# q and k as eight pairs by seven products, with all value columns ahead of them

## The chip, the cores and the metric

The kernel runs on one core of a Trainium2 chip. The metric is device time in microseconds (us) of one launch. The engines are named PE (TensorE, the matmul engine), DVE (VectorE), ACT (ScalarE), POOL (GpSimd) and SP (SyncE, which here only issues DMA transfers).

## The reference, cut to what matters

One step of a hybrid layer on 1024 prompt tokens and 64 new tokens of running streams (T = 1088 columns): an input projection feeds a state-space scan and a differential attention, and a gated mix and a convolutional feed-forward network (FFN) follow. The part that the change touches is

```python
xn = rmsnorm(x) ; proj = xn @ w_in                     # D_MODEL = 1024
z, xbc, dt_raw, q, k, v, gate_ssm, gate_att = split(proj)
q = rope(rmsnorm_per_head(q, q_norm_w))                # 16 heads of 64, q and k 1024 wide each
k = rope(rmsnorm_per_head(k, k_norm_w))                # k is also an output of the step
...
o = diff_attention(q, k_all, v_all)                    # needs all of q, k, v and the cached keys
```

All products are in float32: each operand is split into a high and a low float32r part, and a product is three matmuls (hi hi, lo hi, hi lo) into the same PSUM tile.

## The kernel before, in words

Everything is kept transposed: features on the 128 partitions, the 1088 tokens in the free dimension. `xn` is the normed input, eight feature tiles (KT = 8), held in SBUF as high and low parts in three column ranges `WIDE` of 384, 384 and 320. `weights` loads a block of weights (`w_f`), casts it on ACT (`w_hi`) and subtracts on DVE (`w_lo`). `project` then forms one block of 128 output rows: for each column range 8 x 3 matmuls (L148 to L150) into one bank from `acc`, and a callback `evac` that empties the bank. One call of `next` on it is a "piece" (24 matmuls). A Tile scheduler puts the program into an order for each engine; `tc.high_priority` moves some steps ahead.

The stages, in the order of the program:
1. The input norm, in six column slices (`NORM`); the square sums go over PE (L254). As soon as the first slices are ready, `values(0)` and `values(1)` form the first half of v, together with the raw dt columns.
2. `steps()` turns dt into the decay tables `nacum, decs, dt_tok, dtw` that the scan needs much later; they stay in SBUF.
3. `heads(B_Q, ...)`: the eight row blocks of q one after the other. `evac` copies the bank into a row `qr` in SBUF, squares it on ACT (L325) and adds the square to `ss` on DVE (L326). After the last block a matmul with the block matrix `blk` sums over each head (L335), `rstd_of` (L210 to L214) makes the inverse root, and `finish` multiplies each row (L343), rotates the first two (rope, L352 to L357), splits it (`split_out`: cast on ACT L307, subtraction on DVE L308) and stores the two parts to `q_st`. All rows stay in SBUF meanwhile.
4. `values(2)`, `values(3)`: the other half of v, and the split of the cached keys.
5. `heads(B_K, ...)`: the same for k, which is also stored plain to the output `kT` (L339), then as two parts to `k_st` (L310).
6. Attention, eight heads of nine units (`attend`); head_tiles fetches `q_t, kh_t, kl_t` and others for a head from DRAM (L492). `kh_t` of any head holds rows from all eight row blocks of k, so the first score matmul (L534) comes after the last store of k. Between units `fill(ATT_STEPS)` puts pieces of plain projections (gates `g`, `z`, and the convolution's `xBC`, in `ORDER`) from one stream into PE's queue; they do not depend on attention, and what the stream still has is taken up in the scan. The scheduler also sets plain pieces between k's last product and the first score.
7. The scan, the branches, the output projection, and the FFN, which in both kernels forms its products by a Strassen-Winograd scheme: seven products of half size for eight, 272 columns wide (QW = T / 4).

## Time and profile before

| | |
|---|---|
| median of 3 runs | 2492.93 us (2492.44 to 2493.63) |
| the profiled execution's own time | 2499.35 us |
| its span, first to last instruction | 2497.2 us |
| mean granted clock of PE | 0.993 |
| busy: PE, DVE, ACT, POOL | 2441.4, 1592.7, 1181.6, 691.4 us |
| DMA | 403.62 MB, mean 162 GB/s |

A row of the grouped view reads: line, engine, operation, output<-input, shape, xcount, then busy us and mean ns of one, then the idle time of that engine before them and what ended it. A window's row has for each engine the busy time and (xcount) of its instructions, then the granted clock, the DMA engines' busy share and GB/s. A timeline row has start, duration, engine, line and operation. A row of DMA issues has count, KB of one and the median us from issue to landing. The records of matmuls overlap, since the engine is pipelined: how fast they follow each other is read from their starts or from their number in a full window, not from the duration of one.

### The profile page before, as it was taken

How to read it: one execution, taken by the hardware profiler on the slowest of the kernel's cores; microseconds unless marked ns; L12 is line 12 of the kernel's file. 1: busy time of each engine (PE TensorE's matmuls, PEld its weight loads, DVE VectorE, ACT ScalarE, POOL GpSimd, SP SyncE). 2: the span in 40 equal slices, each digit the busy share in tenths (PEclk: the TensorE clock that was granted, in tenths of full speed). 3: DMA queues.
4: the chain of work that ended last, by engine and by line, in shares of the span. 5: the costliest groups of instructions: out<-in, count | busy, mean ns of one | idle time of the engine just before them, and what ended most of it. 6: DMA issues, size and time to landing. Idle time of an engine off the chain costs nothing. (4 is left out here: it accounts for less than half of the span.)

```text
span 2497.2 us, 44757 instructions
## 1 busy us (share of the span) xinstructions
PE 2441.4 (98%) x16958; PEld 2361.0 (95%) x16958; DVE 1592.7 (64%) x2735; ACT 1181.6 (47%) x2564; POOL 691.4 (28%) x712
## 2 busy tenths in 40 slices
PE   8999999999999999999999999899999999999998
PEld 7999999999999999998889899899999999999998
DVE  7326255865777667537666773655687777777765
ACT  6234343644665555437646663325543333344541
POOL 3000000100111001004324331003466676766435
PEclk9999999999999999999999999999999999999999
DMA  5217248454355353255688753755234343457874
GB/s 166 78 56 272 81 190 277 138 163 142 115 152 144 111 152 107 90 189 171 200 286 272 248 162 108 242 181 175 70 110 141 122 141 123 133 186 217 221 181 152
DMA packets 272152, 403.62 MB, mean 162 GB/s; under 512 B 32544, under 2 KB 206240, under 8 KB 271808
## 3 DMA queue, kind: packets, MB, share of 16 engines
q1 hardware_dynamic: 267328, 391.85, 49.0%
q0 software_dynamic: 4608, 8.91, 2.4%
q8 instruction: 133, 2.18, 0.4%
q14 instruction: 83, 0.68, 0.1%
HBM read 267.11 MB, written 133.56 MB: 160 GB/s over the span
## 5 line engine op out<-in xcount | busy, mean ns | idle before, releaser
L148 PE MATMUL mm<-xn_hi,w_hi 128*128 128x384 f32 (+1 forms) x1416 | 469.9, 332 | 0.9 <-DVE zr L430 0.9
L150 PE MATMUL mm<-xn_hi,w_lo 128*128 128x384 f32 (+1 forms) x1416 | 467.7, 330 | 0.4 <-DVE w_lo L142 0.4
L149 PE MATMUL mm<-xn_lo,w_hi 128*128 128x384 f32 (+1 forms) x1416 | 466.5, 329 | 0.0
L148 PEld LDWEIGHTS mm<-xn_hi,w_hi 128*128 128x128 f32 x1416 | 266.2, 188 | 5.3 <-issue 2.0
L150 PEld LDWEIGHTS mm<-xn_hi,w_lo 128*128 128x128 f32 x1416 | 266.1, 188 | 2.9 <-issue 0.8
L149 PEld LDWEIGHTS mm<-xn_lo,w_hi 128*128 128x128 f32 x1416 | 266.2, 188 | 1.8 <-issue 0.6
L142 DVE TENSOR_TENSOR w_lo<-w_f,w_hi 128x1024 fp32r<-128x1024 f32 (+1 forms) x120 | 151.6, 1264 | 129.5 <-ACT w_hi L141 128.6
L1037 PE MATMUL mx<-n,wh 128*128 128x272 f32 x1092 | 209.5, 289 | 2.1 <-ACT u L1173 1.5
L1037 PE MATMUL mx<-m,w_hi 128*128 128x272 f32 x1050 | 202.8, 290 | 6.4 <-DVE down L1187 3.8
L141 ACT CAST w_hi<-w_f 128x1024 fp32r<-128x1024 f32 (+1 forms) x120 | 125.8, 1049 | 128.6 <-PE mm L149 75.2
L1037 PEld LDWEIGHTS mx<-n,wh 128*128 128x128 f32 x1092 | 171.9, 189 | 2.7 <-ACT u L1173 1.7
L1037 PEld LDWEIGHTS mx<-m,w_hi 128*128 128x128 f32 x1050 | 166.9, 190 | 7.6 <-DVE down L1187 4.2
L1037 PE MATMUL mx<-n,wl 128*128 128x272 f32 x546 | 157.6, 289 | 0.0
L148 PE MATMUL mm<-b_hi,w_hi 128*128 128x384 f32 (+1 forms) x448 | 148.0, 331 | 8.5 <-DVE b_g L192 5.3
L1037 PE MATMUL mx<-m,w_lo 128*128 128x272 f32 x525 | 152.4, 290 | 0.0
L150 PE MATMUL mm<-b_hi,w_lo 128*128 128x384 f32 (+1 forms) x448 | 146.8, 328 | 0.0
L149 PE MATMUL mm<-b_lo,w_hi 128*128 128x384 f32 (+1 forms) x448 | 146.7, 327 | 0.0
L548 ACT ACTIVATE p_t<-sc,mx 128x1024 f32<-128x1024 f32 (+5 forms) x144 | 106.1, 739 | 74.9 <-DVE mx L539 36.7
L459 DVE SCALAR_TENSOR_TENSOR cc<-pre,par,cc 128x384 f32<-128x384 f32 (+1 forms) x216 | 126.6, 586 | 22.9 <-ACT cc L457 17.8
L447 POOL COPY pre<-pre 128x3 f32<-128x3 f32 x48 | 13.2, 274 | 453.7 <-ACT pre L448 330.4
L686 POOL TENSOR_SCALAR_AFFINE_SELECT bc<-bc 128x1024 f32<-128x1024 f32 (+1 forms) x36 | 39.7, 1104 | 261.4 <-ACT e L673 261.4
L840 ACT CAST w_hi<-ws 128x512 fp32r<-128x512 f32 (+1 forms) x64 | 38.8, 607 | 150.9 <-PE mx L1037 106.7
(375 smaller groups left out, 6759.9 us busy)
## 6 DMA issues: line engine op xcount, KB each, us to landing
w_f<-in_win_dram SPq DMA_DIRECT2D x76, 512.0 KB, 3.8
w_f<-in_wup_dram SPq DMA_DIRECT2D x44, 512.0 KB, 3.7
hr<-q_sc SPq DMA_DIRECT2D x70, 272.0 KB, 4.3
bc<-a_sc SPq DMA_DIRECT2D x32, 512.0 KB, 5.8
q_sc<-hb SPq DMA_DIRECT2D x44, 272.0 KB, 2.3
gb<-q_sc SPq DMA_DIRECT2D x44, 272.0 KB, 3.7
x_sc<-cc SPq DMA_DIRECT2D x48, 192.0 KB, 2.2
q_sc<-gb SPq DMA_DIRECT2D x33, 272.0 KB, 2.3
```

Of the source, the lines that this page charges most:

```text
L141: S.copy(hi, w)
L142: V.tensor_tensor(out=lo, in0=w, in1=hi, op=ALU.subtract)
L148: PE.matmul(ps, a_hi, b_hi, start=i == 0, stop=False)
L149: PE.matmul(ps, a_hi, b_lo, start=False, stop=False)
L150: PE.matmul(ps, a_lo, b_hi, start=False, stop=i == n - 1)
L447: G.tensor_copy(pre[:, 0:3], tail)
L459: V.scalar_tensor_tensor(cc[:, :m], pre[:, i : i + m], cw(i), cc[:, :m], ALU.mult, ALU.add)
L548: act(p_t[:n, :nk], sc[c][:n, :nk], AF.Exp, bias=mx[:n, c : c + 1], accum_out=dst)
L686: G.affine_select(bc[:L, :, :L], bc[:L, :, :L], [[0, 8], [1, L]], ALU.is_ge, -1e30, base=0, channel_multiplier=-1)
L840: S.copy(hi, src)
L1037: PE.matmul(ps, w[x][:, c], b[y][:, k], start=start and k == t == 0, stop=k == nk - 1 and t == 2, skip_group_check=not start)
```

## The change

**Values first.** `values(2)` and `values(3)` follow `values(0)` and `values(1)` directly, with the dt steps. `xn` becomes one pair of tiles [128, 8, 1088] instead of three pairs by column range.

**q and k by seven products.** The sixteen row blocks are taken as eight pairs. For each pair `left_blocks` loads the two weight blocks, forms the four sums of the scheme on POOL and splits seven left factors (`split`: ACT, then DVE). The right factors are quarters of `xn` (`X`: b11, b21, b22) and four differences t1 to t4, formed once by `differences` beside the values (nine operations on DVE and three on POOL, on 128x544, four times) and split too. There is no room for t1: it goes to DRAM (`t_sc`), and then takes the place of xn's quarter b12, which is kept in `b_sc` and restored during the last pair (`fourth`). `seven` runs the products, each twice 12 matmuls of 272 columns (L575), and adds the parts in the evacuations (L554, L585, L589).

**Rows go through DRAM.** A finished half row `pre` is squared (ACT), summed (now on POOL) and stored to `r_sc`. `Heads.finish` does the norm (L509 and `rstd_of` on 272 columns), then for 16 half rows: load `raw` (L514; the pool `mid` has two of these tiles), multiply (L516, L518), store the plain row for k (L520), split, store both parts (L524). q's 16 units are stepped seven to a pair beside k's first pairs; k's come after the last pair, beside plain pieces. The split of the cached keys is stepped beside q's pairs.

**Plain pieces.** `fill(FIRST)`, twelve pieces, comes ahead of attention, and `ATT_STEPS` falls from 1.9 to 1.74, so that the total is the same. The dt tables are stored to `d_sc` and loaded again for the scan.

```diff
-ATT_STEPS = 1.9
+ATT_STEPS = 1.74
+FIRST = 12
+LEFT = dict(fa=8, fs=2)
+MID = dict(fu=4, pr=4, cc=4, ss=4, fr=2)
...
-        heads(B_Q, lambda j: wq8[:, j : j + 1], q_st, None)
-        run(values(2))
-        run(values(3))
-        for j in range(KT):
-            ck = row("ck", PAST)
-            load(out=ck, in_=ckT[P * j : P * (j + 1), :])
-            split_out(ck, j, PAST, c_st)
-        heads(B_K, lambda j: col(O_KN + j), k_st, kT)
+        load(out=d_sc, in_=dts.rearrange("p a b c -> p (a b c)"))
...
+        f12, f11 = whole("f12", 0, 2 + s, V), whole("f11", 0, s, G)
+        V.tensor_tensor(out=f11, in0=f12, in1=f11, op=ALU.subtract)
+        f22 = whole("f22", 1, 2 + s, V)
+        t2 = trow("t2f")
+        V.tensor_tensor(out=t2, in0=f22, in1=f11, op=ALU.subtract)
+        part("t2", t2)
+        G.tensor_tensor(out=f12, in0=f22, in1=f12, op=ALU.subtract)
+        part("t3", f12)
+        f21 = whole("f21", 1, s, G)
+        V.tensor_tensor(out=f21, in0=f21, in1=t2, op=ALU.subtract)
+        part("t4", f21)
...
+    for s in range(2):
+        for j in range(2):
+            differences(s, j)
...
+    for f in (2, 3):
+        run(values(f))
...
+        def squares(self, h, t):
+            if h not in self.ss:
+                self.ss[h] = mrow("ss", "ss")[:, :HALF]
+                act(self.ss[h], t, AF.Square)
+            else:
+                sq = mrow("cc", "sq")[:, :HALF]
+                act(sq, t, AF.Square)
+                G.tensor_tensor(out=self.ss[h], in0=self.ss[h], in1=sq, op=ALU.add)
...
+            for h in range(2):
+                for j in range(KT):
+                    x = mrow("fr", "raw")[:, :HALF]
+                    load(out=x, in_=r_sc[self.kind][P * j : P * (j + 1), HALF * h : HALF * (h + 1)])
+                    if j < 2:
+                        V.tensor_tensor(out=x, in0=x, in1=self.ss[h], op=ALU.mult)
+                    else:
+                        V.scalar_tensor_tensor(x, x, self.wcol(j), self.ss[h], ALU.mult, ALU.mult)
+                    if self.plain is not None:
+                        load(out=self.plain[P * j : P * (j + 1), HALF * h : HALF * (h + 1)], in_=x)
+                    hi, lo = (mrow("cc", n, R32)[:, :HALF] for n in ("qh", "ql"))
+                    split(hi, lo, x)
+                    for u, t in enumerate((hi, lo)):
+                        load(out=self.to[D * u + P * j : D * u + P * (j + 1), HALF * h : HALF * (h + 1)], in_=t.bitcast(F32))
+                    yield
...
+        for p, s in begin if n == 0 else both:
+            u.send((p, s))
+            if s == 1:
+                nxt += [x for x in [next(coming, None)] if x is not None]
+                next(finishing, None)
+            if n + 1 == len(order) and (p, s) == (4, 1):
+                fourth(b_sc)
+        left = nxt + list(coming)
+        if (kind, f) == ("q", 6):
+            finishing = chain(finishing, heads["q"].finish())
...
+    run(heads["k"].finish())
+    fill(FIRST)
```

How the order on the engines changes is shown at three places. First PE after k's last product; `ss` is the sum of squares, L335 and L509 are the statistics matmuls. Before:

```order
L150 MATMUL mm<-xn_hi_89,w_lo 128x320
L335 MATMUL st<-ss,con 128x384
L148 MATMUL mm<-xn_hi_85,w_hi 128x384
L149 MATMUL mm<-xn_lo_86,w_hi 128x384
L150 MATMUL mm<-xn_hi_85,w_lo 128x384
L148 MATMUL mm<-xn_hi_85,w_hi 128x384
L149 MATMUL mm<-xn_lo_86,w_hi 128x384
L335 MATMUL st<-ss,con 128x384
```

And with the change:

```order
L575 MATMUL mx<-xn_lo,w_hi 128x272
L575 MATMUL mx<-xn_hi,w_lo 128x272
L509 MATMUL mm<-ss,con 128x272 x2
L509 MATMUL mx<-ss,con 128x272 x2
L156 MATMUL mx<-xn_hi,w_hi 128x384
L157 MATMUL mx<-xn_lo,w_hi 128x384
L158 MATMUL mx<-xn_hi,w_lo 128x384
```

All four statistics matmuls now stand directly behind the last product, with no plain matmul between. Up to the first score matmul, 371 plain matmuls follow; before it was 448.

Second SP, in the middle of k's finish (`g_sc`, `z_sc` and `w_f` are the plain pieces' stores and weights). Before:

```order
L310 DMA k_st<-ql 128x1088
L310 DMA k_st<-qh 128x1088
L339 DMA out_dram<-qr 128x1088
L310 DMA k_st<-ql 128x1088
L431 DMA z_sc<-zr 128x384
L339 DMA out_dram<-qr 128x1088
```

And with the change:

```order
L520 DMA out_dram<-raw 128x544
L524 DMA k_st<-qh 128x544
L520 DMA out_dram<-raw 128x544
L524 DMA k_st<-ql 128x544
L524 DMA k_st<-qh 128x544
L514 DMA raw<-r_k 128x544
L524 DMA k_st<-ql 128x544
L652 DMA z_sc<-zr 128x384
L514 DMA raw<-r_k 128x544
```

The stores are half as wide and twice as many, and between them stand loads of `raw`, each of which needs its tile free, that is the plain store (L520) of two units earlier landed.

Third DVE in the pairs of k (L356 is a split's subtraction, L554 and L589 evacuate a bank). Before there were only the sums of squares and the weight remainders, like

```order
L326 TENSOR_TENSOR ss<-ss,qsq 128x384 x2
L142 TENSOR_TENSOR w_lo<-w_f,w_hi 128x1024
L326 TENSOR_TENSOR ss<-ss,qsq 128x320
L326 TENSOR_TENSOR ss<-ss,qsq 128x384 x2
L326 TENSOR_TENSOR ss<-ss,qsq 128x320
```

With the change, in k's last pair:

```order
L589 TENSOR_TENSOR u_3917<-mx,u_3917 128x272
L518 SCALAR_TENSOR_TENSOR raw<-raw,wq_1847,ss 128x544
L356 TENSOR_TENSOR ql<-raw,qh 128x544
L518 SCALAR_TENSOR_TENSOR raw<-raw,wq_1847,ss 128x544
L356 TENSOR_TENSOR ql<-raw,qh 128x544
L150 TENSOR_TENSOR w_lo<-w_f,w_hi 128x1024
L554 TENSOR_TENSOR pre<-mx,u_3917 128x272 x4
```

Units of q's finish, which wait for their `raw` loads, stand ahead of the evacuations of the pair.

More of the change, by code (lines that the diff above doesn't have):

```diff
@@ L409, in hybrid_layer @@
+    for s in range(2):
+        for j in range(2):
+            differences(s, j)
+    for u in range(2):
+        load(out=b_sc[P * u : P * (u + 1), :].rearrange("p (a t) -> p a t", a=4), in_=xn[u][:, :4, HALF:].bitcast(F32))
+    for f in (2, 3):
+        run(values(f))
+    tt.release()
     s1.close()
-    more = None, 0
-    ahead = AHEAD
+    st.release()
     extra.release()
     extra = None
-    cv_pool = tc.alloc_tile_pool(name="cv", bufs=1, side="right")
+    lp = tc.alloc_tile_pool(name="lp", bufs=1)
@@ new lines, in seven, with pile @@
+    def seven(to, left):
+        u1, u2 = to.u1, to.u2
+        banks = {}
+        def pile(key, p, s, start):
+            if start:
+                banks[key, s] = acc(QW)
+            ps, w, b = banks[key, s], left[p], X[PARTS[p], s]
+            for k in range(4):
+                c = slice(P * k, P * (k + 1))
+                for i, (x, y) in enumerate(((0, 0), (0, 1), (1, 0))):
+                    PE.matmul(ps, w[x][:, c], b[y][:, k], start=start and k == i == 0, stop=k == 3 and i == 2,
+                              skip_group_check=not start)
+            return ps
+        at = yield
+        for _ in range(14):
+            p, s = at
+            if p == 0:
+                S.copy(u1[:, s], pile("a", p, s, True))
+            elif p == 1:
+                V.tensor_tensor(out=u2[:, s], in0=pile("b", p, s, True), in1=u1[:, s], op=ALU.add)
+            elif p == 2:
+                to.take(0, 0, s, pile("a", p, s, False), None)
+            elif p == 3:
+                V.tensor_tensor(out=u1[:, s], in0=pile("b", p, s, False), in1=u1[:, s], op=ALU.add)
+            elif p == 4:
+                to.take(1, 1, s, pile("c", p, s, True), u1)
+            elif p == 5:
+                to.take(1, 0, s, pile("d", p, s, True), u1)
+            else:
+                to.take(0, 1, s, pile("c", p, s, False), u2)
+            at = yield
@@ L653, in hybrid_layer @@
         more = psi, 1
+        dts = sp.tile([P, 4, 9, 32], F32, name="dts")
+        nacum, decs, dt_tok, dtw = (dts[:, i] for i in range(4))
+        dtt = dts[:, 2:]
+        load(out=dts, in_=d_sc.rearrange("p (a b c) -> p a b c", a=4, b=9))
         def fetch(g, c, w):
```

274 lines of the change are left out of this document (194 added, 80 removed).

## The prediction

> **What bounds the kernel now.** I read the page's engine table first, then windows over the stages that the change touches, then the waits of TensorE (PE) there.
>
> ```profile
> PE 2441.4 (98%) x16958; PEld 2361.0 (95%) x16958; DVE 1592.7 (64%) x2735; ACT 1181.6 (47%) x2564; POOL 691.4 (28%) x712
> ```
>
> PE is busy 98 % of the span and no other engine passes 64 %. So the change is worth what it takes off PE, minus what it leaves PE waiting for. The windows (columns as their header line says, PE first) tell how full PE is in each stage.
>
> ```profile
> core 0: us, PE busy (x) PEld busy (x) DVE busy (x) ACT busy (x) POOL busy (x), PEclk, DMA share, GB/s
> 84.80:99.90 15.10, 15.10 (x92) 14.61 (x91) 8.92 (x18) 1.83 (x4) 0.00 (x0) 1.00 0.42 148
> 182.00:235.00 53.00, 53.00 (x437) 52.31 (x436) 35.01 (x38) 23.63 (x40) 0.00 (x0) 1.00 0.71 259
> 240.00:320.00 80.00, 80.00 (x488) 80.00 (x487) 20.55 (x30) 26.07 (x54) 0.10 (x1) 1.00 0.26 91
> 325.00:410.00 85.00, 83.63 (x499) 81.68 (x498) 47.15 (x66) 33.39 (x51) 0.00 (x0) 1.00 0.73 262
> 350.00:390.00 40.00, 38.68 (x233) 38.09 (x232) 30.19 (x35) 13.26 (x18) 0.00 (x0) 1.00 1.02 389
> 410.00:1099.00 689.00, 686.02 (x4405) 659.66 (x4404) 466.91 (x1010) 372.91 (x936) 48.33 (x143) 1.00 0.46 137
> 2000.00:2100.00 100.00, 100.00 (x800) 100.00 (x799) 72.14 (x103) 39.13 (x70) 69.25 (x67) 1.00 0.42 138
> ```
>
> Values 2 and 3 run at 182 to 235, the k products at 240 to 320, k's norm, split and stores at 325 to 410, attention at 410 to 1099; 2000 to 2100 lies in the FFN, which already uses seven products of 272 columns. PE idles only in k's finish (1.4 us in 85) and in attention (3.0 in 689). The DMA engines are full at one place: 350 to 390, share 1.02, 389 GB/s. The k finish is hidden at present, and I needed to see how. SP's and PE's timelines (start, duration):
>
> ```profile
> 388.46 0.32 SPq L310 DMA_DIRECT2D k_st<-ql  x1
> 397.00 1.50 SPq L492 DMA_DIRECT2D q_t<-q_st  x3
> 398.55 2.52 SPq L492 DMA_DIRECT2D kh_t<-k_st  x4
> 408.29 0.39 PE L534 MATMUL sc<-kh_t,q_t 128*128 128x512 f32 x1
> ```
>
> The last split store of k is issued at 388.46, the first head's keys are fetched from 398.55, and the first score matmul is at 408.29, 9.7 us after that fetch began. Between k's last product (about 330) and that score PE works through 448 plain matmuls. They cover it with only this left:
>
> ```profile
> PE mm L148 <- DVE zr L430: 0.9, 1, 0.9
> PE mm L150 <- DVE w_lo L142: 0.4, 1, 0.4
> ```
>
> **The change, part by part.** *The products.* Each old block of q or k is 72 matmuls of 384 or 320 columns, 16 blocks make 1152. By the window 240:320 one takes 80.00/488 = 163.9 ns, so 188.8 us. Each pair is now 7 products x 2 halves x 12 matmuls of 272 columns, eight pairs make 1344; by the window 2000:2100 one takes 100/800 = 125.0 ns, so 168.0 us. Gain **-20.8 us**. An eighth less arithmetic would be 23.6; the rest is lost because a narrow matmul costs more per column (0.460 against about 0.452 ns). A lost record in either window moves this by about 1 us.
>
> *The start.* PE's order now has 16 statistics matmuls of 192 columns ahead of the first value product, before 8.
>
> ```profile
> 15.03 2.12 PE L254 MATMUL st<-nsq,con 128*128 128x192 f32 x8 [0.43 <-ACT nsq L253]
> 17.38 1.83 PE L254 MATMUL st<-nsq,con 128*128 128x192 f32 x8 [0.23 <-ACT nsq L253]
> 19.74 0.40 PE L148 MATMUL mx<-w_hi,xn_hi 128*128 128x272 f32 x1 [0.53 <-ACT w_hi L141]
> ```
>
> One slice of the norm is 2.35 us (15.03 to 17.38), during which nothing else is ready: **+2.4**, between 0 (the slices that overlap products later get shorter by as much) and 5 (two slices).
>
> *The differences, beside values 2 and 3.* They must be ready when the first pair starts; the cover is the 53.0 us of those values, while q's 8 blocks used to lie between. VectorE gets 4 x 9 operations on 128x544, the dt steps (the window 84.80:99.90 holds only these on DVE, 8.92) and three weight remainders; GpSimd gets 12 additions.
>
> ```profile
> L352 DVE TENSOR_TENSOR t<-qr,rp x4: 718/718/720, 205.7 to 364.8; 128x544 f32<-128x544 f32 x4
> L142 DVE TENSOR_TENSOR w_lo<-w_f,w_hi 128x1024 fp32r<-128x1024 f32 x116 | 146.4, 1263 | 129.5 <-ACT w_hi L141 128.6 <-DMA out_dram<-x 0.5
> L1008 POOL TENSOR_TENSOR ge<-gb,gb 128x544 f32<-128x544 f32 x11 | 15.4, 1404 | 15.0 <-DMA gb<-q_sc 15.0
> L1011 POOL TENSOR_TENSOR gb<-gb,gb 128x544 f32<-128x544 f32 x11 | 18.8, 1705 | 0.8
> L841 DVE TENSOR_TENSOR w_lo<-ws,w_hi 128x512 fp32r<-128x512 f32 x56 | 47.8, 854 | 4.7 <-ACT w_hi L840 2.1
> L841 DVE TENSOR_TENSOR w_lo<-w_f,w_hi 128x512 fp32r<-128x512 f32 x28 | 41.3, 1476 | 3.8 <-ACT w_hi L840 3.8
> L841 DVE TENSOR_TENSOR wl<-w_f,wh 128x512 fp32r<-128x512 f32 x84 | 76.7, 914 | 19.3 <-ACT wh L840 18.7
> ```
>
> DVE: 36 x 0.718 + 8.92 + 3 x 1.263 = 38.6 us. POOL: 12 x 1.55 (between 1.404 and 1.705) = 18.6. Side by side that is under 53. But the three L841 rows show one operation on one shape at 854, 914 and 1476 ns, the slow form where POOL is adding to the same weights: the two engines hold each other up. Laid end to end they are 57.2, and the rest of dt (about 2 us of copies) follows: 59.2 - 53.0 = **+6**, between 0 (they overlap) and 14 (the first pair's four weight sums on POOL and four splits come behind as well). The Trainium skill, "SBUF — State Buffer", section "Who interferes with whom", says that a VectorE operation with two SBUF inputs and a GpSimd operation that reads SBUF wait for each other whole. By that rule alone this term is the +6, by plain overlap it is 0; the 1476 agrees with it, the 854 shows that it seldom hits.
>
> *q's finish, beside k's pairs.* The norm no longer works on rows that lie in SBUF. Sixteen half rows are read back from DRAM into two `raw` tiles, and VectorE's queue holds the multiply, which waits for that load, ahead of the pair's evacuations. Rows for the loads and stores (count, KB, median us to landing) and for the cast:
>
> ```profile
> hr<-q_sc SPq DMA_DIRECT2D x70, 272.0 KB, 4.3
> xr<-out_dram SPq DMA_DIRECT2D x16, 272.0 KB, 5.6
> out_dram<-down SPq DMA_DIRECT2D x16, 272.0 KB, 2.2
> out_dram<-x SPq DMA_DIRECT2D x32, 136.0 KB, 3.2
> kh_t<-k_st SPq DMA_DIRECT2D x32, 272.0 KB, 8.0
> ...
> L1024 ACT CAST m<-hr 128x544 fp32r<-128x544 f32 x40 | 25.5, 647 | 13.6 <-DMA hr<-q_sc 13.4
> ```
>
> A tile of q turns over in load 4.3, multiply 0.72, cast 0.65 and remainder 0.72: 6.4, up to 7.7 with a load of 5.6. Two tiles give a unit per 3.2 to 3.9 us, and seven units per pair need 22 to 27 us against 168 x 125 ns = 21.0 of products. Eight PSUM banks absorb part; I take **+5**, between 0 and 12 (two pairs at 27).
>
> *k's finish.* This is the term that decides. Nothing of it lies beside products; it has the plain pieces alone, and of those PE's order now has 371 matmuls between the statistics and the first score, 371 x 163.9 = 60.8 us. The chain from the last product to the first score:
> - The last evacuation with its square and sum (0.44 as the L1140 row under the rivals has it, a square of 544 as long as the cast's 0.65, then a POOL addition of 1.4 to 1.7): 3.0 with the waits between.
> - The norm of the first half, two statistics tiles:
>
> ```profile
> 331.76 0.58 ACT L210 ACTIVATE qn<-st,eps_t 128x384 f32<-128x384 f32 x1
> 334.08 0.56 DVE L214 SCALAR_TENSOR_TENSOR qrs<-qn,qn 128x384 f32<-128x384 f32 x1
> 339.35 1.28 ACT L210 ACT_TABLE_LOAD   x1 [1.26 <-DVE qrs L214]
> ```
>
>   One takes 334.64 - 331.76 = 2.9, two 5.8, and a table load brings it to 6.5 or so.
> - Eight rounds of two units. The next load into a tile waits for the store of the plain row out of it, so a round is load, two multiplies in turn, store and an issue. At the lowest rows 4.3 + 0.72 + 2.2 = 7.2; at the highest 5.6 + 2 x 0.72 + 3.2 = 10.2. I take 9.0 (load 5.0, between its two rows, 1.4, store 2.3, issue 0.3): the stage moves at least 2.2 MB per round (eight transfers of 278,528 bytes), which alone is 5.7 us at the 389 GB/s of the full window above, so loads will land late. The first load is issued before the products end: 8 x 9.0 - 5.0 = 67.0.
> - The last split store 2.3, then from the fetch to the score 9.7.
>
> Sum 3.0 + 6.5 + 67.0 + 2.3 + 9.7 = 88.5; minus 60.8 of cover and the 1.3 that PE waits already: **+26.4**. In general it is 8 x round - 45.6, so 12 at 7.2 and 36 at 10.2. It may show at plain pieces too, since their weight remainders stand behind the multiplies on DVE and their weight loads behind stores that wait on SP; the sum is the same.
>
> The Trainium skill, "DMA: Bandwidth & Descriptors", section "Anatomy of one DMA — SWDGE (gpsimd) path", gives 2.0 us and bytes at 436 GB/s for a transfer, so 2.6 us here; with load and store at that, a round is about 6.7 and this term 8 (an estimate). It is fitted on another queue; the 2.2 of the store row agrees, the 4.3 and 5.6 of the load rows do not.
>
> *Attention* gets 1.74 pieces per unit for 1.9: 72 x 0.16 = 11.5 pieces fewer, the twelve that went ahead. PE idles 3.0 us there with DVE busy 467 of 689; as much again is **+2**, between 0 and 6. The dt tables' way through DRAM (590 KB) is issued far ahead of the scan: 0, at most 1. Cached keys only move. The stored t1 and the restored b12 are 2.2 MB each, 5.7 us at 389 GB/s; t1 is wanted after five products (15 us), b12 after two products and the first plain piece (10 us): 0.
>
> **Sum:** -20.8 + 2.4 + 6 + 5 + 26.4 + 2 = +21.0. The profiled execution took 2499.35 for a span of 2497.2, and its median sister runs 2492.9; the difference carries over, so 2492.9 + 21.0 = **2514**. About 0.2 % (5 us) is what a measurement of this kernel can tell from no change.
>
> **Rivals.** *Hidden after all (the other sign).* If a round is 5.7 us or less, 8 x round - 45.6 is nothing and k's finish stays under the plain pieces. With half of the small terms (7.7) the change gives -20.8 + 7.7 = -13: 2480. The sum changes sign at a round of 6.4 with the small terms, at 8.3 without any. For it: stores land in 2.2, the present stage is hidden. Against it: 2.2 MB per round plus the plain pieces' weights and stores fill the DMA engines as 350 to 390 did, and no load row is under 4.3. Chance 0.10.
>
> *The DMA engines stay full.* Loads queue behind 544-wide stores and a round is 11: 42.4 for k's finish, +37 in all, 2530. For it: share 1.02 already without the 4.5 MB of rows that are read back; 8.0 us for 272 KB of keys. Against it: only two loads are out at a time. Chance 0.17.
>
> *DVE and POOL throttle the pairs.*
>
> ```profile
> L1140 DVE TENSOR_TENSOR hb<-mx,u 128x272 f32<-128x272 f32 x30 | 13.1, 439 | 21.7 <-PE mx L1037 20.6 <-issue 0.9
> ```
>
> A k pair with q's units has 10 evacuations x 0.44, 7 splits x 0.85, 14 operations x 0.72 on DVE (20.4) and some eight x 1.45 on POOL (11.6): 32 end to end against 21.0. Two such pairs are +20 instead of +5: 2529. Against it: the FFN window holds 103 DVE and 67 POOL operations in 100 us with PE at 100. Chance 0.15.
>
> **Chances.** Forecast 0.58, the three rivals 0.10, 0.17, 0.15. The forecast's own ends are -20.8 + 12 = -9 with no small term and +52 with all at their highest; 8 in 10 lie in 2490 to 2543, which takes in both slower rivals and leaves out most of the fast one. Faster by over 0.2 % is the first rival nearly alone, 0.10; within it 0.08; slower 0.82.
>
> **What would show it.** Right: 272-column matmuls at 125 ns in the pairs; a gap of 20 to 35 us in PE before the first score or at the plain pieces just ahead of it, released by DMA or DVE; `raw` loads at 4 to 6 us and rounds near 9 us on SP. Wrong: PE without gaps between k's last product and attention, or a loss of more than 10 us in the pairs themselves or in attention.

## The result and the profile after

| | before | after |
|---|---|---|
| runs, us | 2492.68 median, 2490.31 to 2493.63 | **2549.67** median, 2546.22 to 2554.1 |
| ratio of the runs | | 1.0231, 95 % interval 1.0213 to 1.0249 |
| profiled execution / its span, us | 2499.35 / 2497.2 | 2546.22 / 2544.4 |

The change makes the kernel 57 us slower; the forecast was 21 slower and ended its range at 2543. The spans differ by 47.2. The other 10 come from which executions were profiled: that of before lay 6.7 above its median, that of after 3.5 below.

The engine table of after, first:

```profile
PE 2433.2 (96%) x17154; PEld 2351.0 (92%) x17154; DVE 1678.5 (66%) x2885; ACT 1206.7 (47%) x2616; POOL 804.0 (32%) x784
```

PE is busy 8 us less than before in a span that is 47 longer. So the products did get cheaper, and the loss is waiting, with half-speed running behind some of the waits. The windows of after (columns as before: PE busy first, then the granted clock) stand for values 2 and 3, q's pairs, k's pairs, the finish of k, attention, and 100 us of the FFN:

```profile
core 0: us, PE busy (x) PEld busy (x) DVE busy (x) ACT busy (x) POOL busy (x), PEclk, DMA share, GB/s
90.80:152.70 61.90, 56.60 (x454) 55.22 (x453) 53.60 (x67) 21.43 (x45) 30.05 (x16) 0.97 0.30 100
152.70:244.50 91.80, 86.22 (x675) 84.69 (x674) 57.74 (x87) 37.38 (x72) 42.43 (x29) 1.00 0.59 205
244.50:342.40 97.90, 89.42 (x682) 88.20 (x680) 72.29 (x115) 44.50 (x85) 35.45 (x25) 0.97 0.72 246
342.40:441.40 99.00, 67.56 (x381) 66.11 (x380) 38.10 (x66) 30.51 (x55) 4.81 (x5) 0.83 0.91 296
441.40:1130.00 688.60, 686.17 (x4409) 661.95 (x4408) 465.08 (x997) 371.65 (x928) 46.29 (x143) 1.00 0.44 130
2030.00:2130.00 100.00, 99.97 (x798) 99.75 (x797) 74.84 (x109) 40.99 (x75) 65.71 (x67) 1.00 0.39 126
```

Attention and the FFN are as full as before. PE idles 5.3 us in values 2 and 3, 14.1 in the pairs, 31.4 in k's finish, and here the clock falls below 1.00, which it did in none of the windows read of before. The account by stage, from the first matmul of each stage to that of the next:

| stage | before | after | difference | forecast |
|---|---|---|---|---|
| start to first value product | 19.7 | 27.6 | +7.9 | +2.4 |
| values 0 and 1 | 63.4 | 63.2 | -0.2 | 0 |
| values 2 and 3 (after: with about 2 us of dt) | 53.3 | 61.9 | +8.6 | +6 |
| products of q and k | 193.6 | 189.7 | -3.9 | -15.8 |
| last product to first score | 78.2, 448 plain matmuls | 99.0, 371 plain | +20.8 and 12.6 for the 77 put off | +26.4 |
| first score to the end | 2088.9 | 2103.0 | +14.1, 12.6 of it those 77 | +2 |

The waits of TensorE between 80 and 445 us of after name the places (line waited for, us in total, times, longest):

```profile
PE mm L156 <- DVE zr L651: 26.7, 1, 26.7
PE mx L575 <- DVE pre L554: 7.4, 2, 5.4
PE mm L156 <- ACT w_hi L149: 5.1, 1, 5.1
PE mm L509 <- POOL ss L487: 4.7, 1, 4.7
```

*The long one.* The timelines of PE, ACT and SP at its end:

```profile
434.38 0.63 PE L156 MATMUL mm<-xn_hi,w_hi 128*128 128x320 f32 x1 [26.69 <-DVE zr L651]
...
433.13 0.87 ACT L650 ACTIVATE zr<-mm 128x384 f32<-128x384 f32 x2 [7.60 <-DMA k_st<-ql]
...
427.47 1.35 SPq L524 DMA_DIRECT2D k_st<-ql  x1
432.34 2.37 SPq L722 DMA_DIRECT2D kh_t<-k_st  x4
```

PE waits for the evacuation of a plain piece, which waits not for a result but for k's *last store*: the staging tile of the pieces after the first twelve (`FIRST`) lies in space that the finish's tiles hold until that store has landed. The store is issued at 427.47 and has landed before 433.13. ACT empties the banks of twelve pieces between 357 and 404 us, and that of the thirteenth at 433.13. So the plain pieces that can be finished under k's finish are those twelve, whatever the order lists behind them: 336 of the 371 matmuls run before the wait, 35 after it.

*The rounds of the finish*, by VectorE's multiplies (the first and the last shown) and the DMA issues (count, KB, median us to landing):

```profile
352.39 1.36 DVE L516 TENSOR_TENSOR raw<-raw,ss 128x544 f32<-128x544 f32 x2
...
424.02 0.78 DVE L518 SCALAR_TENSOR_TENSOR raw<-raw,par,ss 128x544 f32<-128x544 f32 x1 [3.48 <-DMA raw<-r_k]
```

```profile
raw<-r_k SPq DMA_DIRECT2D x16, 272.0 KB, 4.5
out_dram<-raw SPq DMA_DIRECT2D x16, 272.0 KB, 2.9
k_st<-ql SPq DMA_DIRECT2D x16, 272.0 KB, 4.2
```

From the first unit's multiply to the sixteenth's it is 71.6 us, seven and a half rounds of two units, 9.5 us each. The forecast took 9.0.

*The clock.* PE's timeline at the end of the last pair:

```profile
331.01 0.42 PE L575 MATMUL mx<-t,w_hi 128*128 128x272 f32 x2
331.27 0.29 PE L575 MATMUL mx<-t,w_lo 128*128 128x272 f32 x1
337.00 0.59 PE L575 MATMUL mx<-xn_hi,w_hi 128*128 128x272 f32 x1 [5.44 <-DVE pre L554]
337.39 0.43 PE L575 MATMUL mx<-xn_lo,w_hi 128*128 128x272 f32 x1
337.62 0.43 PE L575 MATMUL mx<-xn_hi,w_lo 128*128 128x272 f32 x1
...
342.32 0.29 PE L575 MATMUL mx<-xn_hi,w_lo 128*128 128x272 f32 x1
347.35 2.18 PE L509 MATMUL mm<-ss,con 128*128 128x272 f32 x4 [4.75 <-POOL ss L487]
```

Before the wait of 5.44 us the matmuls start 0.13 us apart (two from 331.01 to 331.27), behind it 0.23 apart (337.39 to 337.62), up to 342.15, for 5 us. A wait can thus cost more than its length.

### The profile page after: what moved, and what is told of

It reads as the page before. It is cut to its first block, busy times and chain, and to the rows that moved or that the text cites. A ratio compares the mean times of both kernels' runs of the same rounds, so it can differ in the third digit from the quotient of the medians.

```text
span 2544.4 us, 45910 instructions
## 1 busy us (share of the span) xinstructions
PE 2433.2 (96%) x17154; PEld 2351.0 (92%) x17154; DVE 1678.5 (66%) x2885; ACT 1206.7 (47%) x2616; POOL 804.0 (32%) x784
## 5 line engine op out<-in xcount | busy, mean ns | idle before, releaser
L156 PE MATMUL mm<-xn_hi,w_hi 128*128 128x384 f32 (+1 forms) x1632 | 549.3, 337 | 36.7 <-DVE zr L651 26.7
L158 PE MATMUL mm<-xn_hi,w_lo 128*128 128x384 f32 (+1 forms) x1632 | 541.1, 332 | 0.0
L157 PE MATMUL mm<-xn_lo,w_hi 128*128 128x384 f32 (+1 forms) x1632 | 540.9, 331 | 0.0
L156 PEld LDWEIGHTS mm<-xn_hi,w_hi 128*128 128x128 f32 x1632 | 309.4, 190 | 45.9 <-DVE zr L651 27.0
L157 PEld LDWEIGHTS mm<-xn_lo,w_hi 128*128 128x128 f32 x1632 | 309.3, 190 | 5.5 <-issue 3.8
L158 PEld LDWEIGHTS mm<-xn_hi,w_lo 128*128 128x128 f32 x1632 | 308.9, 189 | 1.6 <-issue 1.0
L149 ACT CAST w_hi<-w_f 128x1024 fp32r<-128x1024 f32 (+1 forms) x104 | 109.0, 1048 | 75.6 <-PE mm L157 49.0
L1074 ACT CAST w_hi<-ws 128x512 fp32r<-128x512 f32 (+1 forms) x64 | 38.9, 607 | 148.8 <-PE mx L1270 91.8
L1297 POOL TENSOR_TENSOR hb<-hb,cc 128x480 f32<-128x480 f32 (+2 forms) x66 | 92.4, 1413 | 42.1 <-ACT w_hi L1074 21.7
L1270 PEld LDWEIGHTS mx<-m,w_lo 128*128 128x128 f32 x534 | 100.8, 189 | 0.0
L1270 PEld LDWEIGHTS mx<-n,wl 128*128 128x128 f32 x534 | 100.3, 188 | 0.0
```

Source lines behind the costliest of these rows:

```text
L149: S.copy(hi, w)
L156: PE.matmul(ps, a_hi, b_hi, start=i == 0, stop=False)
L157: PE.matmul(ps, a_hi, b_lo, start=False, stop=False)
L158: PE.matmul(ps, a_lo, b_hi, start=False, stop=i == n - 1)
L1074: S.copy(hi, src)
L1270: PE.matmul(ps, w[x][:, c], b[y][:, k], start=start and k == t == 0, stop=k == nk - 1 and t == 2, skip_group_check=not start)
```

## The experiments

Ratios are to the kernel before on the same chip; the changed kernel stands at 1.0231. e1 to e6 are each one edit of the changed kernel; from e7 on the base is e2.

**e1, more plain pieces ahead of attention.**

```diff
-ATT_STEPS = 1.74
-FIRST = 12
+ATT_STEPS = 1.6
+FIRST = 22
-ORDER = (("g", (15, 14)), ("z", range(4)), ("c", group(0)), ("g", range(13, 7, -1)), ("c", group(1)), ("c", group(2)),
-         ("z", range(4, 8)), ("c", group(3)), ("z", range(8, 16)), ("g", range(7, 1, -1)))
+ORDER = (("g", (15, 14)), ("z", range(8)), ("c", group(0)), ("g", range(13, 7, -1)), ("c", group(1)), ("c", group(2)),
+         ("c", group(3)), ("z", range(8, 16)), ("g", range(7, 1, -1)))
```

> Twenty-two plain pieces ahead of the swap of PE's staging pool instead of twelve (and 1.6 per attention unit, so the same total; the z blocks 4 to 7 come earlier in the stream). Theory A (PE stops in k's finish because the plain pieces run out: the thirteenth needs a staging tile in the space of the pool that k's last stores still read): the 26.7 us gap at 407 to 434 fills with ten pieces of 3.9 us, the half-speed matmuls behind it go, time -25 to -29, about 2522. Theory B (the finish is bound by full DMA engines): ten more pieces bring about 3.6 MB, at 320 to 390 GB/s 9 to 11 us more on the chain, so only -15 to -18, about 2533. Theory C (attention misses those pieces): PE idles in attention instead, less than -10.

Measured 2524.48 us, ratio 1.0138 (1.0119 to 1.0156). The largest wait of TensorE from 345 to 456 us:

```profile
PE mm L509 <- POOL ss L487: 4.6, 1, 4.6
```

The 26.7 us wait is gone, the time falls by 23 (by the ratios). The wait was a lack of pieces that can run, not of engines.

**e2, tiles of its own for k's finish.**

```diff
+            own = lambda tag, name, dt=F32, n=6: mrow(tag, name, dt) if pool is None else pool.tile([P, MIDW], dt, name=name, tag=tag, bufs=n)
...
-                    x = mrow("fr", "raw")[:, :HALF]
+                    x = own("fr", "raw")[:, :HALF]
...
-                    hi, lo = (mrow("cc", n, R32)[:, :HALF] for n in ("qh", "ql"))
+                    hi, lo = (own("cc", n, R32, 12)[:, :HALF] for n in ("qh", "ql"))
...
-    run(heads["k"].finish())
+    kf = tc.alloc_tile_pool(name="kf", bufs=1)
+    run(heads["k"].finish(kf))
```

So `raw` has six tiles for two, the split twelve for four.

> k's finish gets tiles of its own, six for the rows read back and twelve for their two parts, in the space that the differences leave, instead of two and four; nothing else changes. Theory A (a round of two units is a chain of latencies: load 4.5, multiply, store 2.9, issue): with six tiles the rounds overlap, 10.1 us per round falls to 6 or less, the finish ends 25 us or more earlier and PE's gap goes: -25 or more. Theory B (the DMA engines are full from 365 on, share 0.96 to 1.05): 17.8 MB of k and some 5 MB of plain pieces need 60 us at 389 GB/s, so the finish shortens by 10 to 15 us at most: -10 to -15.

Measured 2514.5 us, ratio 1.0093 (1.0078 to 1.0108). Windows over the pairs and over the finish, then the evacuation of the thirteenth plain piece, the last split store and the fetch:

```profile
151.30:340.80 189.50, 174.98 (x1354) 172.32 (x1352) 129.04 (x202) 81.43 (x157) 76.44 (x52) 0.98 0.65 224
340.80:425.90 85.10, 79.31 (x468) 78.24 (x467) 41.09 (x71) 32.41 (x60) 7.37 (x6) 0.96 0.93 327
...
402.34 0.49 ACT L651 ACTIVATE zr<-mm 128x384 f32<-128x384 f32 x1 [2.74 <-PE mm L158]
404.08 0.32 SPq L525 DMA_DIRECT2D k_st<-ql  x1
417.32 2.51 SPq L725 DMA_DIRECT2D kh_t<-k_st  x4
```

The last store is issued at 404.08, 63 us after the last product (85 before the edit), and 468 matmuls run under the finish in place of 381. The same bytes go faster with more tiles, so the rounds were a chain through two tiles, not a full DMA system: the rival "the DMA engines stay full" falls. No long wait for `zr` is left, but not for the number of tiles alone. The edit also moves them: they now lie in a pool of their own, not in the space that the later staging tiles take over. The thirteenth piece is evacuated at 402.34, before k's last store is even issued, so the staging tiles no longer wait for that store. The 34 us (by the ratios) are the worth of both, number and place, and were not separated; e1 shows that the wait for that space alone was worth 23.

**e3, k's pairs ahead of q's**, so that q's finish stands alone at the end.

```diff
-    order = [(n, f, f + 1) for n in "qk" for f in range(0, KT, 2)]
+    order = [(n, f, f + 1) for n in "kq" for f in range(0, KT, 2)]
...
-        if (kind, f) == ("q", 6):
-            finishing = chain(finishing, heads["q"].finish())
+        if (kind, f) == ("k", 6):
+            finishing = chain(finishing, heads["k"].finish())
...
-    run(heads["k"].finish())
+    run(heads["q"].finish())
```

> k's four pairs go first and q's after them, so that k's finish (with the plain store) runs beside q's pairs and q's finish (without it) stands alone. Theory A (the plain store's landing holds a raw tile, and its bytes fill the DMA engines): a round of q is load 4.5, multiply 0.8, cast 0.65, remainder 0.72, about 7 us, so the finish is 8 x 3 = 24 us shorter, while the pairs lose up to 10 more, since k's slower units stand ahead of q's evacuations: -10 to -20. Rival (only the last stores and the fetch of a head set the end): within 5 of the change.

Measured 2542.3 us, ratio 1.0205 (1.0189 to 1.0221), some 6 us less than the changed kernel where 10 to 20 were expected, with overlapping intervals: q's finish, which has no plain store, ends sooner (84.5 us from the last product to the score), but k's, beside q's pairs, holds those longer. The largest wait of TensorE from 150 to 440 us:

```profile
PE mx L575 <- DVE pre L554: 21.1, 3, 17.6
```

**e4, q's units thinner**, four per pair of k for seven.

```diff
-                next(finishing, None)
+                if kind == "q" or p % 2 == 0:
+                    next(finishing, None)
```

> q's finish is stepped four units to a pair over all four pairs of k, instead of seven to a pair. Theory A (k's pairs stall because DVE's queue holds a unit that waits for its load ahead of the evacuations): the gaps of 1.7, 1.2 and 5.4 us in k's pairs change place but shrink by half, -4 to -6, unless the last units then delay k's own last rows. Rival (the gaps come from DVE and POOL holding each other up, which does not depend on the units): within 2 of the change.

Measured 2558.79 us, ratio 1.0274 (1.0256 to 1.0292). The pairs take 184.8 us, 4.9 less, the finish 114.6, 15.6 more. TensorE's wait for `zr` has grown to 43.3 us: what no longer stands beside the last pairs delays the finish by more than the pairs gain.

**e5, the differences' additions and subtractions on VectorE.**

```diff
-        f12, f11 = whole("f12", 0, 2 + s, V), whole("f11", 0, s, G)
+        f12, f11 = whole("f12", 0, 2 + s, V), whole("f11", 0, s, V)
...
-        G.tensor_tensor(out=f12, in0=f22, in1=f12, op=ALU.subtract)
+        V.tensor_tensor(out=f12, in0=f22, in1=f12, op=ALU.subtract)
...
-        f21 = whole("f21", 1, s, G)
+        f21 = whole("f21", 1, s, V)
```

> The three operations of each call of differences that GpSimd does go to VectorE (36 becomes 48 operations of 0.72 on DVE, none on POOL). Theory A (DVE and POOL hold each other up whole): DVE's operations that took 1.4 to 1.9 us beside POOL fall to 0.72; the stage of values 2 and 3 (61.9 us) and the 5.1 us gap at 123.7 shrink, -2 to -6. Rival (no exclusion that counts; DVE is simply the engine with the most work there): DVE gets 8.6 us more, the stage grows by 5 to 9.

Measured 2539.63 us, ratio 1.0213 (1.0196 to 1.0231): by this edit alone the medians do not separate. The trace does. Groups of instructions between 90 and 153 us, first of the changed kernel, then of this one (columns: busy, mean ns):

```profile
L377 DVE TENSOR_TENSOR f<-xn_hi,xn_lo 128x544 f32<-128x544 f32 x8 | 6.8, 862 | 2.1 <-PE mm L158 2.1
L388 DVE TENSOR_TENSOR t2f<-f,f 128x544 f32<-128x544 f32 x4 | 5.2, 1291 | 0.0
```

```profile
L377 DVE TENSOR_TENSOR f<-xn_hi,xn_lo 128x544 f32<-128x544 f32 x16 | 10.9, 711 | 2.1 <-PE mm L158 2.1
L388 DVE TENSOR_TENSOR t2f<-f,f 128x544 f32<-128x544 f32 x4 | 2.8, 710 | 0.0
```

The same operations on the same shapes take 862 and 1291 ns beside GpSimd and 710 without it. VectorE's busy time in the stage falls from 53.60 to 44.32 us (90 to 145.6 in e5), though it has twelve operations more. The 5.1 us wait in values 2 and 3 is gone, and the pairs begin at 145.6 for 152.7. The +6 that the forecast took from laying the two engines end to end is this; GpSimd's own operations (2164 ns for an addition of this shape) left the chain with the same edit, and that share was not separated.

**e6, the first value products at high priority.**

```diff
-            product(ps, [(hi[:, k], lo[:, k],
-                          w2[k // 4][0][:, k % 4], w2[k // 4][1][:, k % 4]) for k in range(KT)])
+            with tc.high_priority(quick or 0):
+                product(ps, [(hi[:, k], lo[:, k],
+                              w2[k // 4][0][:, k % 4], w2[k // 4][1][:, k % 4]) for k in range(KT)])
```

> The products of values 0 and 1 get the same priority as their evacuations, so that PE's order has them behind the second norm slice's statistics, as before the change, instead of behind the fourth's; nothing else is edited. Theory A (the change lost 7.9 us at the start because PE waited, in order, for the squares of slices 3 and 4): the first product comes at about 20, the half-speed matmuls until 37 shrink, -6 to -9. Rival (the norm itself limits the start, PE only waits elsewhere for later slices): within 3 of the change.

Measured 2548.79 us, ratio 1.0236 (1.0221 to 1.0251), no gain. But the edit did not bring the order that it was meant to bring. The first product comes at 26.99 for 27.60, and in both traces it stands behind the statistics of four norm slices; before the change it stood behind three. So neither theory was tested, and whether TensorE's order holds the start back stays open.

**e7 and e8, e2 with two plain pieces ahead of the statistics.** e8 has besides e6's edit, the last pair's sums of squares on VectorE (`V if self.tail else G`) and five of q's units per pair of k for seven.

```diff
     kf = tc.alloc_tile_pool(name="kf", bufs=1)
+    fill(2)
     run(heads["k"].finish(kf))
-    fill(FIRST)
+    fill(FIRST - 2)
```

> As the kernel with own tiles for k's finish (e2_deep), and two plain pieces go ahead of k's statistics in the program. Theory A (the 5.8 us that PE waits for the last sums of squares cost a second time, because the matmuls after a gap of 5 us run at half speed for some 3.5 to 5 us): gap and slow matmuls go, -7 to -8 against e2_deep, so about 2507. Rival (the gap alone counts, or the work is only shifted and the first score waits longer): -3 to -6, or nothing.

> All mends together: own tiles for k's finish, two plain pieces ahead of its statistics, the last pair's squares summed on VectorE, q's units five to a pair instead of seven, products early at the start. If the terms are independent: -35 (own tiles) -7 (statistics) -7 (start) -3 to -5 (pairs), about 2497, still 4 to 8 above the kernel before, since the pairs keep 10 us or more of stalls and the values stage its 8. If the pairs' stalls come from the units alone, 2490 or less.

Measured 2526.2 (1.0149, 1.0134 to 1.0165) and 2527.66 (1.0154, 1.0139 to 1.0169), 12 and 13 worse than e2. The waits of e7 from 325 to 436 us, and one of ACT from 376 to 418:

```profile
PE mm L156 <- DVE zr L652: 12.7, 1, 12.7
ACT zr L651 <- DMA z_sc<-zr: 12.7, 2, 7.1
```

The wait for the sum of squares is filled, but a wait at the staging tile is back. It is not the one of 26.7 us: here ACT waits for the pieces' own earlier stores (`z_sc`), which are issued between those of k's finish, and all of it lies before k's last store (416.97). So filling one gap early opened another. That the two pieces spent early are what is missing there is a reading; no run shows it.

**e9 to e12, on the base of e2.** e9: the differences on VectorE as in e5. e10: 48 matmuls that feed nothing, ahead of the first value product:

```diff
+                if x == 1:
+                    busy(6, xn[0][:, k, c : c + w])
```

Here `busy` is six matmuls on the row just written into a bank that nobody reads. e11: 44 such matmuls ahead of the finish's statistics:

```diff
+    ps = acc(QW)
+    for i in range(44):
+        PE.matmul(ps, xn[0][:, 5, :P], xn[0][:, 6, :QW], start=i == 0, stop=i == 43)
     run(heads["k"].finish(kf))
```

e12: e2, e9 and e10 together.

> The kernel with k's finish on tiles of its own (2514.5), and the differences' GpSimd subtractions on VectorE. Theory A (GpSimd and VectorE hold each other up beside values 2 and 3): the 5 us gap in the values goes, the pairs begin some 5 to 7 us earlier, and the time falls by what the same edit gave the changed kernel, 4.5 to 10: 2504 to 2510. Rival B (that gain is lost again in the pairs, which wait for the weight sums and evacuations anyway): pairs begin earlier and are longer by as much, 2512 to 2516.

> The same kernel with 48 matmuls that feed nothing, laid into TensorE's wait ahead of the first value product, nothing else. Theory A (a pause of about 5 us drops the granted clock, and the first 35 or so products at 227 ns in place of 125 are on the path): products at 125 ns from the first, values 0 and 1 end about 3.5 us earlier, 2511. Rival B (VectorE's norm and weight remainders set the start, the slow clock is hidden): clock 1.00 but the values end where they did, 2514 to 2516.

> The same kernel with 44 matmuls that feed nothing, laid into TensorE's waits at the end of the last pair (5.7 and 5.8 us in the profile), nothing else. Theory A (the clock drops after those waits): the 32 or so products and the four statistics matmuls behind them run at full clock (the statistics in 0.5 us each in place of 1.0), first score 4 us earlier, 2510.5. Rival B (the evacuations and squares, not TensorE, set that stage): full clock but the first score where it was, 2514 to 2517.

> All parts that should help: k's finish on tiles of its own, differences on VectorE, matmuls that feed nothing in the wait ahead of the first value product. If each is worth what its own theory says, 2500 to 2506; if the rivals hold, 2512 to 2515. By either it stays slower than the kernel before, 2492.7, since k's finish still defers what the plain matmuls no longer cover.

| | us | ratio |
|---|---|---|
| e9 | 2508.83 | 1.0073 (1.0060 to 1.0085) |
| e10 | 2512.66 | 1.0095 (1.0079 to 1.0112) |
| e11 | 2521.67 | 1.0127 (1.0111 to 1.0143) |
| e12 | 2505.14 | 1.0062 (1.0050 to 1.0075) |

e9 gains 5, as expected; its interval overlaps that of e2, but in its trace the pairs begin at 144.4 for 151.3. e10 shows the clock. A window of it, and behind that the same one of e2:

```profile
30.00:32.00 2.00, 2.00 (x18) 2.00 (x17) 2.00 (x4) 0.18 (x1) 2.00 (x1) 1.00 0.86 267
```

```profile
30.00:32.00 2.00, 2.00 (x11) 2.00 (x11) 2.00 (x3) 0.94 (x2) 2.00 (x1) 0.50 0.76 227
```

Useless work in the wait keeps the clock at 1.00. What it is worth is less: the work itself puts the first product off (28.40 for 25.94), the pairs begin at 149.9 for 151.3, and the intervals of e10 and e2 overlap. e11 is a miss: the scheduler laid 30 of the 44 into the last pair and plain pieces between the statistics, so the edit was not one edit, and its loss of 7 says nothing about the clock.

**e13 to e15, what holds the pairs?** e13 is e12 with q's finish behind the last pair too, on the same tiles as k's, and FIRST and ATT_STEPS of e1. e14 has 30 pieces ahead (1.49 per unit). e15 is e13 with the cached keys' split moved behind k's finish, so that nothing is left beside the pairs.

```diff
-        if (kind, f) == ("q", 6):
-            finishing = chain(finishing, heads["q"].finish())
+    run(heads["q"].finish(kf))
     run(heads["k"].finish(kf))
```

> The best version so far (2505.1; pairs 183.5 us) with q's norm and split taken out from beside k's pairs: they run after the last pair, on the finish's own tiles, ahead of k's; 22 plain pieces go ahead of attention in place of 12 (1.6 per unit in attention). Cached keys stay beside q's pairs. Theory A (VectorE's queue, whose multiply waits for a row on its way from DRAM, holds the pairs' evacuations): k's four pairs, 94.5 us now, take 21.1 each as the one pair that has nothing beside it, 84 to 87; 32 units then need about 30 MB of transfers, 90 us at 340 GB/s, under some 600 plain matmuls of 98 us: 2495 to 2503. Rival B (evacuations and weight sums limit the pairs by themselves): k's pairs stay over 91 and the longer finish is added, 2508 to 2520.

> The same with 30 plain pieces ahead of attention (1.49 per unit). If the finish is a chain that 22 pieces don't cover, 5 to 10 us faster than with 22; if it is covered, the same within 3 us or a little slower, as attention has fewer pieces to fill with.

> The version with 22 pieces, and the cached keys' split also moved behind k's finish, so that the pairs have nothing beside them. Theory A: all eight pairs at 21.0 to 21.3 us, 170 in all (q's four were 89.4 with the cached keys beside the first two); 2 to 4 us faster than with the cached keys beside q's pairs, unless the eight units lengthen the finish by as much. Rival B: the first pairs stay at 22 to 25, since their weights and sums are what they wait for.

Measured 2513.08 us (1.0085, 1.0063 to 1.0108), 2502.11 (1.0046, 1.0031 to 1.0062) and 2513.8 (1.0095, 1.0072 to 1.0117). Windows over k's pairs of e12, then over q's pairs and k's pairs of e13, then of e15:

```profile
233.00:328.00 95.00, 88.57 (x681) 87.39 (x680) 71.58 (x114) 43.52 (x84) 33.93 (x23) 0.98 0.68 237
```

```profile
144.90:233.00 88.10, 84.08 (x665) 83.19 (x664) 60.32 (x90) 38.89 (x75) 46.74 (x31) 1.00 0.59 210
233.00:320.20 87.20, 85.86 (x684) 85.47 (x683) 50.28 (x77) 32.04 (x59) 38.56 (x27) 1.00 0.35 120
```

```profile
143.00:229.00 86.00, 85.38 (x679) 84.94 (x678) 57.28 (x84) 35.77 (x68) 44.91 (x32) 1.00 0.43 152
229.00:314.50 85.50, 84.15 (x670) 83.76 (x669) 49.16 (x75) 31.59 (x59) 37.53 (x26) 1.00 0.34 120
```

Without q's units k's pairs take 87.2 for 95.0, without the cached keys q's take 86.0 for 88.1. Alone, eight pairs take 171.5, 3.5 over the 168 of their matmuls; GpSimd is as busy as in e13 or e12. So the units beside the pairs cause 12 us of loss (183.5 in e12), not the pairs' own sums and evacuations. Whether it is more VectorE's waiting for rows or the 21 us of work that the units give it (71.58 for 50.28 in k's pairs) was not separated. The time is then lost in a finish of twice the length: with 22 pieces PE waits 12.0 us for `zr` (e13), with 30 it waits 3.2 there and 5.2 for the first keys (e14). e14 has the lowest median of all the variants, about 11 us over before; its interval overlaps that of e12. No version beat the kernel before.

## Why the prediction was wrong, step by step

The sign and the main term were right: the products got cheaper by about the stated 21 (171.5 us alone in e15 for 193.6 before), and k's finish gives that back and more. The size was less than half. Against the spans' 47.2 the sum of +21.0 lacks 26:

- **Products and q's finish, +12 too low.** Measured are 91.8 us for q's pairs and 97.9 for k's, for 84 of matmuls each: 21.7 above the matmuls where +5 was taken. (Before took 193.6 for the 188.8 of the sum, so 12 of the missing 16.7 show as a difference.) The forecast said itself that a loss of more than 10 us in the pairs would show it wrong. The mechanism was named there, a multiply that waits for its row ahead of the evacuations in VectorE's queue, but it was priced for two pairs of k alone. The steps that failed are "Eight PSUM banks absorb part; I take **+5**", which measured 13.9 in k's pairs, and "Cached keys only move", with which q's pairs were put at nothing and measured 7.8. The waits of VectorE from 288 to 343 us:

```profile
DVE raw L518 <- DMA raw<-r_q: 7.2, 5, 2.7
```

  Five such multiplies wait 7.2 us in all, and PE 14.1 over both halves of the pairs. In q's pairs the cached keys also load, cast and subtract on DVE; by e15 against e13 they are 2 of q's 7.8. The rest of the 7.8 was not taken apart. And behind the wait of 5.4 us the clock was down.
- **k's finish, 7 too low.** 26.4 was forecast, 33.4 measured. Round: 9.0 taken, 9.5 measured. Last sum of squares: 3.0 taken, 4.9 measured (342.4 to 347.35). Last store: 2.3 taken, about 5 measured (427.47 to the release before 433.13). From the fetch to the score 9.7 taken, 9.1 measured. The sum came near for a partly wrong reason: the 371 matmuls of cover do not run evenly under the chain, they stop when the staging tile is wanted, and the last 35 run at the end, after a 26.7 us pause, the first 3 us of them at half clock. Counting the work that the order lists behind a chain is not enough; its tiles must be free while the chain runs.
- **The start, 5.5 too low.** The forecast had one more norm slice ahead of the first product, which is right, but took half a slice for a whole one. Its two rows at 15.03 and 17.38 are the halves of one slice, since each of the eight statistics matmuls of a slice leaves two records: the three slices of 192 columns have 48. That slice lasts from 15.03 to the next at 20.00, about 5 us for the 2.35 taken. The count, from the trace before, and the fourth slice in the trace after, which begins at 20.43 with the last two of the ten records of its first row:

```profile
L254 PE MATMUL st<-nsq,con x96: 270/326/553, 5.7 to 51.8; 128*128 128x192 f32 x48, 128*128 128x128 f32 x32, 128*128 128x256 f32 x16
...
18.62 2.40 PE L261 MATMUL st<-nsq,con 128*128 128x192 f32 x10 [0.50 <-ACT nsq L260]
...
26.22 0.59 PE L261 MATMUL st<-nsq,con 128*128 128x192 f32 x2 [1.32 <-POOL nsq L258]
27.60 0.39 PE L156 MATMUL mx<-w_hi,xn_hi 128*128 128x272 f32 x1 [0.78 <-ACT w_hi L149]
```

  From 20.43 to the product at 27.60 it is 7.2 of the measured 7.9. Why this slice takes 7.2 and not 5 was not tried.
- **Values and differences, 2.6 too low**, of which 2 are dt's own matmuls, which merely moved here. e5 confirms the cause: the two engines hold each other up.
- **Attention**, forecast +2, measured +1.5.
- **"The difference carries over"**, 10 us. The prediction added the sum to the median of before as if the profiled executions stood the same way to their medians. They did not.

Of the rivals, "DMA engines stay full" is refuted by e2, "hidden after all" by the result. "DVE and POOL throttle the pairs" had the right place and, at +20 over the products, the right size. e15 shows that GpSimd's sums alone do not hold the pairs; whether they also slow the units beside them was not separated (q's multiply takes 967 ns on average in k's pairs of the changed kernel, and 779 in the late finish of e15). The loss came *with* the forecast's finish term, not in its place. Terms in different stages can go wrong together, and the range, built of one rival at a time, left no room for that.

On the two rules weighed there: the Trainium skill, "SBUF — State Buffer", section "Who interferes with whom", has VectorE and GpSimd wait for each other whole; e5's pairs of rows (1291 and 710 ns) agree on the direction, and the mean of 862 says that only some of those operations meet one of GpSimd's. The figure of the Trainium skill, "DMA: Bandwidth & Descriptors", section "Anatomy of one DMA — SWDGE (gpsimd) path", came to 2.6 us for 272 KB; here the finish's loads took 4.5, its plain stores 2.9.

## What to carry to other kernels

A chain that is hidden under other work is hidden only by work whose inputs, banks and staging tiles are free at that moment: check the pool that the cover writes to, not just the order. Operations that wait for memory must not stand on an in-order engine ahead of the evacuations that TensorE waits for; if they cannot be moved, give them more tiles, and tiles that do not lie where the next stage's staging goes (both in one edit here: 34 us). And a cheaper product is worth its saving only as far as the way of its rows through DRAM stays hidden; here that way cost more than the 21 us saved. And a row of a timeline may hold two records of one instruction: count them against the program before a stage is priced from it.

## What was unexpected of the hardware

The granted clock falls after waits, but not by their length alone. Matmuls then run at half speed (272 columns: 227 ns for 127). Every wait of 3.63 us and more between two matmuls in these 17 traces, before and after included, had the granted clock at 0.50 within 1.5 us of its end; waits of 3.22 (e14) and 2.65 (e10) did too, waits of 3.45 (e2), 3.62 (e4), 3.03 (e9) and 2.59 (e10) did not. The Trainium skill, "TensorE: Matmul & The Clock Gate", section "HAM oscillation — how this bites in real kernels", puts the limit at about 3.4 us of idle; the runs agree with the order of size, not with a sharp limit there.

The clock's own records in these traces tell more. In each of them it changes only on a fixed grid of 3.41 us, and a half-speed stretch is one or more whole steps long, mostly 3.41 or 6.83 us. Behind a full-speed step in which PE was busy, by its records, for under 0.4 of the time, the next step was at half speed in 135 of 135 cases; behind one with over 0.6 in 5 of some 11 900; between them in 41 of 141. So it matters how a wait falls on the grid. Three steps of e4 with its wait of 3.62 us, which is split over the first two, and two steps of e10 with its wait of 2.65, which lies mostly in the first:

```profile
305.80:309.20 3.40, 1.61 (x13) 1.40 (x12) 3.40 (x4) 0.07 (x1) 2.66 (x2) 1.00 0.10 34
309.20:312.60 3.40, 1.57 (x12) 1.56 (x12) 3.40 (x6) 2.19 (x4) 1.35 (x1) 1.00 0.61 199
312.60:316.00 3.40, 3.37 (x27) 3.16 (x26) 2.97 (x7) 1.67 (x4) 0.32 (x1) 1.00 1.03 369
```

```profile
336.40:339.80 3.40, 1.07 (x9) 0.86 (x7) 2.01 (x5) 1.78 (x4) 3.40 (x3) 1.00 1.01 325
339.80:343.20 3.40, 3.07 (x10) 3.10 (x11) 2.02 (x1) 1.80 (x4) 3.40 (x3) 0.50 1.04 406
```

e10's window at 30 us shows that matmuls without use keep the rate up. And the kernel before had such stretches too, here behind a wait of 5.35 us in a later stage:

```profile
1577.50:1580.00 2.50, 2.41 (x8) 2.44 (x9) 2.43 (x6) 0.60 (x2) 0.00 (x0) 0.50 1.07 368
```

This row lay in the trace that the prediction was made from, outside the windows that it read. With it, each new wait of some microseconds in the sum would have been charged 2 us or so more (an estimate: half of the 3.4 to 5.2 us that matmuls ran at half speed behind the waits of the changed kernel up to the first score).
